# Router on the tokens between the two norms, first tile routed and half gathered before the second is made

## The chip, the cores and the metric

The kernel runs on one core of a Trainium2 chip. The metric is device microseconds of one execution, taken as the median of several runs. The core has a matrix engine (TensorE: PE for its matmuls, PEld for its weight loads), a vector engine (VectorE, DVE), a scalar engine (ScalarE, ACT), a general engine (GpSimd, POOL), a sync engine (SyncE, SP) that here issues nearly all transfers, and 16 DMA engines that carry them. Matmul results land in PSUM, which has 8 banks; everything else on the core lives in SBUF.

## The reference

Two layers over 256 tokens of width 1024. Each layer mixes tokens (attention of 8 heads beside a causal pooling mixer, one output projection), then runs a mixture of 16 experts:

```python
x = layer_norm_affine(DEEPNORM_ALPHA * x + g1 * y, ln1_g[l], ln1_b[l])      # "first norm"
h = layer_norm_plain(x) * (1 + sc2) + sh2                                   # "second norm"
...
scores = jax.nn.softmax((hf @ w_router).astype(jnp.float32), axis=-1)
sel = scores + router_bias
grp = sel.reshape(-1, N_EXPERT_GROUPS, EXPERTS_PER_GROUP)
best = jnp.argmax(lax.top_k(grp, TOP_K)[0].sum(-1), axis=-1)
...                                        # the two best experts of the best group, weights summing to 1
for e in range(N_EXPERTS):
    a = jax.nn.silu(hf @ w_gate[e]) * (hf @ w_up[e])
    y = y + gates[:, e:e + 1] * (a @ w_down[e])
```

`sh1, sc1, g1, sh2, sc2, g2` are the six parts of `silu(c) @ w_mod[l] + b_mod[l]`, called `mod` parts 0 to 5 below. A plain norm is (x - mean) / deviation per token, so the router's product with h is, per token, (x @ (sc * w) - mean * column sums of sc * w) / deviation + sh2 @ w, with sc = 1 + sc2.

## The kernel before

All weights are read once, 278.6 MB in pieces of 1 MB or less. `Stream` holds them in the order of use; `pump` issues the next piece on SP's queue whenever fewer than `limit` pieces are held, and `free` gives a piece back as soon as the matmul that uses it last is written down. The pieces live in a ring of 21 slots (`NS`) that also lends slots to scratch tiles: the rows `G`, `B` of the first norm, the normed tokens `xn2`, their transposes `xnT`. SP's queue works in order: an issue whose slot is still being read holds all that follow it.

Each engine works through its own list in the order in which the program was written (`manual_schedule`); engines wait for one another only for data and buffers. The tokens are two tiles `t` of 128. At the end of `mixer`:

- `out_mm(t)` is the output projection; the second tile's ends in two halves of 256 columns, and with its last columns the four `out` weight pieces are freed. `norms_of(t)` adds the residual, makes the first norm into `xt[:, t]` and the second into `xn2[t]`.
- `turn(t)` transposes `xn2[t]`, `logits(t)` multiplies by the router's weights, `exps(t)` sums the partial products and takes the exponentials.
- `xh`, `xl` are two parts of `xn2` whose sum is used in the gather, each for both tiles.
- `mod_mm(l, 5)` and `mod_mm(l + 1, 1)` (the latter in layer 0 only) multiply the condition by pieces of `w_mod`. They stand between `logits(0)` and `turn(1)`. `gate` (from `mod_fin(l, 5)`) runs `spread`: four matmuls and two ACT copies that lay the gate row over all partitions.

Then `router` runs `gate()`, makes the top-2 mask `M` of both tiles in one chain of small DVE operations, and places the tokens with three matmuls against a triangle (`posm`). `experts` makes one-hot tiles of 8 experts, gathers (`gather(0)`: 8 banks, four matmuls each, `xh` and `xl` of both tiles) and goes through eight pairs of experts: `gate_up`, `silu` (a tanh on ACT, two DVE products), `act_t`, `down`, `combine`. `warm(n)` is n matmuls of ones with no reader.

Layer 1 begins with `mod_mm(1, 0)`, whose weights come last in layer 0's stream; `mod_fin(1, 0)` then turns its result into columns, with a DVE sum that stands ahead of the DVE work on the second norm of the new layer (`ready`).

Of the kernel before, what the change touches and what calls it, by code (L numbers as in the profile page):

```python
# [8 lines left out]
F = mybir.dt.float32  # L9
BF = mybir.dt.bfloat16  # L10
# [6 lines left out]
D = 1024  # L17
# [56 lines left out]
def tile_trunk(ctx, tc, x, c, w_mod, b_mod, w_in, w_pool, pool_scale, w_out, ln1_g, ln1_b,  # L74
# [251 lines left out]

    def mod_fin(l, v):
        acc = macc.pop((l, v))
        part = s2()
        A.copy(part, acc)  # L330
        if v == 5:
            return lambda: spread(l, v, [(selm[:, n:n + 1], part) for n in range(2)])
        b = ps()
# [112 lines left out]
    def mixer(l, hT, xn, ready):  # L446
# [162 lines left out]

        py = [[], []]  # L610

        def out_mm(t):
            for n in range(2):
                last = t == 1 and n == 1
                for m in range(2 if last else 1):
                    c0, c1 = (256 * m, 256 * m + 256) if last else (0, 512)
                    py[t].append(ps())
                    for q in (2, 3, 0, 1):
                        w = st.get(("out", l, q))
                        for kk in range(2):  # L620
                            k = 2 * q + kk
                            T.matmul(py[t][-1][:, 0:c1 - c0], catT[:, k, t * 128:(t + 1) * 128],  # L622
                                     w[:, kk, n * 512 + c0:n * 512 + c1],
                                     start=(q == 2 and kk == 0), stop=(q == 1 and kk == 1))
                        if last and m:
                            st.free(("out", l, q))
# [6 lines left out]
        def norms_of(t):  # L633
            z = xn2[t]
            nb, wd = (4, 256) if t else (2, 512)
            bn = tiny.tile([128, nb, 6], F, name=f"bn{nb}")
            for j, (a, b) in enumerate(((0, 512), (512, 768), (768, D)) if t else ((0, 512), (512, D))):
                c0 = slice(a, b)
                V.tensor_mul(z[:, c0], py[t][j][:, 0:b - a], g1[:, c0])
                V.scalar_tensor_tensor(z[:, c0], xt[:, t, c0], ALPHA, z[:, c0], op0=OP.mult, op1=OP.add)  # L640
                for i in range(a // wd, b // wd):
                    V.bn_stats(bn[:, i, :], z[:, i * wd:(i + 1) * wd])
            affine(xt[:, t], z, z, G, B, stats_end(bn))

            mv, rs = stats(xt[:, t])
            V.tensor_scalar(z.rearrange("p (k q) -> p k q", k=8), xt[:, t].rearrange("p (q k) -> p k q", k=8),
                            mv[:, 0:1], rs, op0=OP.subtract, op1=OP.mult)

        def turn(t):
            for h in range(2):  # L650
                b = ps()
                for k in range(4):
                    T.transpose(b[:, k * 128:(k + 1) * 128], xn2[t][:, (4 * h + k) * 128:(4 * h + k + 1) * 128], ident)
                A.copy(xnT[:, 4 * h:4 * h + 4, t * 128:(t + 1) * 128], b.rearrange("p (k s) -> p k s", k=4))

        out_mm(0)
        norms_of(0)
        xh = big.tile([128, 2, D], FR, name="xn")

# [19 lines left out]
        A.copy(xh[:, 0], xn2[0])  # L679
# [3 lines left out]
        out_mm(1)  # L683

        bb = ps()
        for k in range(8):
            j = k % 4
            T.matmul(bb[32 * j:32 * j + 32, 0:1], wr[:, k, :], sh2[:, k:k + 1], start=(k < 4), stop=(k >= 4))
        rbias = const.tile([128, 1], F, name="rbias", bufs=1)
        A.copy(rbias, bb[:, 0:1])  # L690
        rpart = s2(S)

        def logits(t):
# [5 lines left out]
            A.activation(rpart[:, t * 128:(t + 1) * 128], bl[:, 0:128], AF.Identity, bias=rbias)  # L699

        xl = big.tile([128, 2, D], FR, name="hT")

        turn(0)
        logits(0)
        pl = ps()
        lg = [pl[:, t * 16:t * 16 + 16] for t in range(2)]
        ex = tiny.tile([128, 2, 16], F, name="r_ex", bufs=1)
        mx = tiny.tile([128, 2], F, name="r_mx", bufs=1)
        sm = tiny.tile([128, 2], F, name="r_sm", bufs=1)

        def exps(t):
            T.matmul(lg[t], rpart[:, t * 128:(t + 1) * 128], sel16[:, 0:NE], start=True, stop=True)
            V.tensor_reduce(mx[:, t:t + 1], lg[t], axis=AX.X, op=OP.max, negate=True)
            A.activation(ex[:, t], lg[t], AF.Exp, bias=mx[:, t:t + 1], accum_out=sm[:, t:t + 1])

        mod_mm(l, 5)
        gate = mod_fin(l, 5)
        if l + 1 < DEPTH:
            mod_mm(l + 1, 1)
        norms_of(1)  # L720
        exps(0)
        if l + 1 == DEPTH:
            warm(7)

        V.tensor_sub(xl[:, 0], xn2[0], xh[:, 0].bitcast(F))
        V.tensor_copy(xh[:, 1], xn2[1])
        V.tensor_sub(xl[:, 1], xn2[1], xh[:, 1].bitcast(F))
        turn(1)
        logits(1)
        exps(1)  # L730
        return xh, xl, (mx, ex, sm), gate
# [43 lines left out]
    def router(l, mes, gate):  # L775
        def tn(shape, name, dt=F):
            return tiny.tile([128] + shape, dt, name=name, bufs=1)

        mx, ex, sm = mes
        gate()  # L780
        warm(6)
# [431 lines left out]
```

## Time and profile before

| what | value |
|---|---|
| time, median of 3 runs | 725.13 us (724.12 to 725.71) |
| time of the profiled execution | 724.93 us |
| span of the profiled execution | 723.1 us |
| busy share PE / DVE / ACT / POOL | 94% / 45% / 17% / 7% |
| read from HBM | 278.59 MB, 387 GB/s over the span |
| output stage of the mixer to the first expert pair, layer 1 | 468.08 to 507.08 us |

The profiled execution's time is 1.8 us above its span and 0.2 us under the median. Layer 0 goes to about 366 us; the same stage of layer 0 lies 348.75 us before that of layer 1. A busy share is an average over stages with different limits, and a matmul's end is modelled, so a PE at 94% says little by itself.

### The profile page before, as it was taken

What the parts mean: (1) busy time and instruction counts of PE and PEld (TensorE: products, weight loads), DVE (VectorE), ACT (ScalarE), POOL (GpSimd) and SP (SyncE); (2) the same over time, 40 slices, a digit from 0 to 9 for tenths busy, and PEclk for the clock granted to TensorE, in tenths of its full rate; (3) what the DMA queues carried; (4) which work ended last, traced back from release to release, by engine and by line L of the source; (5) the groups of instructions that cost most, each with busy time, mean ns of one, the idle gap of its engine ahead of it and who ended that gap; (6) DMA issues with size and microseconds to landing.
All of it is one profiled execution on the core that took longest, in us unless ns stands there. A gap on an engine that the chain in (4) does not pass through costs nothing. (4 is left out here: it accounts for less than half of the span.)

```text
span 723.1 us, 8334 instructions
## 1 busy us (share of the span) xinstructions
PE 678.9 (94%) x3213; PEld 316.8 (44%) x3218; DVE 326.8 (45%) x582; ACT 124.8 (17%) x268; POOL 49.7 (7%) x76
## 2 busy tenths in 40 slices
PE   5999899999999999989979999998999999998994
PEld 2447555553333533423324575555333344342331
DVE  4008897662332532413153966666323243241305
ACT  1011432130110210121002035213210011012100
POOL 5001501100000000000010051010000000000002
PEclk9999999999999999999989999999999999999998
DMA  9999999999999999999999999767699999999992
GB/s 307 366 384 409 408 409 420 373 421 392 424 420 420 422 421 421 420 416 418 395 406 392 409 410 406 310 272 301 282 420 422 421 424 419 420 422 418 418 395 77
DMA packets 61729, 280.37 MB, mean 388 GB/s; under 512 B 5008, under 2 KB 14264, under 8 KB 38632
## 3 DMA queue, kind: packets, MB, share of 16 engines
q1 hardware_dynamic: 61040, 279.20, 96.1%
q8 instruction: 30, 0.49, 0.3%
q10 hardware_dynamic: 312, 0.32, 0.1%
q0 software_dynamic: 320, 0.14, 0.1%
q14 instruction: 27, 0.22, 0.1%
HBM read 278.59 MB, written 1.05 MB: 387 GB/s over the span
## 5 line engine op out<-in xcount | busy, mean ns | idle before, releaser
L918 PE MATMUL ps<-wr 128*64 128x512 f32 x1024 | 226.1, 596 | 0.0
L918 PEld LDWEIGHTS ps<-wr 128*64 128x64 f32 x1024 | 73.5, 138 | 147.2 <-issue 142.3
L960 PE MATMUL ps<-wr,s 128*64 128x512 f32 x512 | 113.8, 595 | 3.7 <-DVE s L945 2.9
L960 PEld LDWEIGHTS ps<-wr,s 128*64 128x64 f32 x512 | 35.5, 137 | 72.0 <-issue 63.8
L970 DVE SCALAR_TENSOR_TENSOR s<-ps,gc,gb 128x512 f32<-128x512 f32 x32 | 24.0, 748 | 84.0 <-PE ps L960 84.0
L455 PE MATMUL ps<-wr,hT 128*128 128x512 f32 x128 | 57.0, 597 | 0.4 <-ACT hT L429 0.2
L361 DVE SCALAR_TENSOR_TENSOR wr<-wr,condT 128x1024 f32<-128x1024 f32 x42 | 55.8, 1329 | 2.3 <-DMA wr<-in_w_mod_dram 0.9
L622 PE MATMUL ps<-wr,hT 128*128 128x512 f32 (+1 forms) x160 | 55.7, 507 | 0.1
L389 POOL TENSOR_TENSOR rs<-rs,mhalf 128x1 f32<-128x1 f32 x16 | 13.2, 823 | 554.1 <-DVE rs L388 554.1
L935 DVE TENSOR_TENSOR s<-s,ps 128x512 f32<-128x512 f32 x16 | 11.0, 687 | 86.5 <-PE ps L918 86.5
L973 ACT CAST wr<-s 128x512 fp32r<-128x512 f32 x30 | 18.5, 618 | 164.7 <-PE ps L918 107.7
L974 DVE TENSOR_TENSOR wr<-s,wr 128x512 fp32r<-128x512 f32 x30 | 20.8, 692 | 55.6 <-ACT wr L973 55.6
L622 PEld LDWEIGHTS ps<-wr,hT 128*128 128x128 f32 x160 | 30.2, 190 | 23.8 <-issue 21.5
L455 PEld LDWEIGHTS ps<-wr,hT 128*128 128x128 f32 x128 | 23.6, 190 | 28.9 <-issue 27.1
L984 PE MATMUL ps<-wr,sT 128*128 128x512 f32 x120 | 33.6, 413 | 0.0
L578 PE MATMUL ps<-wr,hT 128*128 128x512 f32 x64 | 28.3, 595 | 0.0
L504 PE MATMUL ps<-hT,wr 128*128 128x256 f32 x128 | 28.1, 380 | 0.0
L984 PEld LDWEIGHTS ps<-wr,sT 128*128 128x128 f32 x120 | 20.9, 189 | 16.3 <-issue 13.0
L933 DVE SCALAR_TENSOR_TENSOR s<-s,ps 128x512 f32<-128x512 f32 x16 | 11.0, 685 | 36.7 <-ACT s L932 36.7
L504 PEld LDWEIGHTS ps<-hT,wr 128*128 128x128 f32 x128 | 24.2, 190 | 4.5 <-issue 1.3
L876 PE MATMUL ps<-s,xn 128*128 128x512 f32 x64 | 25.4, 398 | 0.3 <-DVE s L854 0.3
L996 DVE TENSOR_TENSOR xt<-xt,ps 128x512 f32<-128x512 f32 x40 | 25.2, 683 | 0.5
(240 smaller groups left out, 611.5 us busy)
## 6 DMA issues: line engine op xcount, KB each, us to landing
wr<-in_w_gate_dram SPq DMA_DIRECT2D x64, 1024.0 KB, 19.3
wr<-in_w_up_dram SPq DMA_DIRECT2D x60, 1024.0 KB, 19.3
wr<-in_w_down_dram SPq DMA_DIRECT2D x56, 1024.0 KB, 19.5
wr<-in_w_mod_dram SPq DMA_DIRECT2D x48, 1024.0 KB, 15.1
wr<-in_w_in_dram SPq DMA_DIRECT2D x16, 1024.0 KB, 15.1
wr<-in_w_out_dram SPq DMA_DIRECT2D x8, 1024.0 KB, 18.7
wr<-in_w_down_dram SPq DMA_DIRECT2D x12, 512.0 KB, 11.1
wr<-in_w_up_dram SPq DMA_DIRECT2D x8, 512.0 KB, 17.4
```

What stands on the lines that cost most here:

```text
L361: V.scalar_tensor_tensor(acc, w[:, kk], condT[:, k, 0:1], acc, op0=OP.mult, op1=OP.add)
L455: T.matmul(pq[t][n], hT[:, k, t * 128:(t + 1) * 128], w[:, kk, n * 512:(n + 1) * 512], start=(k == 0), stop=(k == 7))
L504: T.matmul(pp[g // 2][:, (g % 2) * 256:(g % 2) * 256 + 256], w[:, kk, g * 128:(g + 1) * 128], hT[:, k, :], start=(k == 0 and g % 2 == 0), ...
L578: T.matmul(pv[t], hT[:, k, t * 128:(t + 1) * 128], w[:, kk, :], start=(k == 0), stop=(k == 7))
L622: T.matmul(py[t][-1][:, 0:c1 - c0], catT[:, k, t * 128:(t + 1) * 128], w[:, kk, n * 512 + c0:n * 512 + c1], start=(q == 2 and kk == 0), st ...
L876: T.matmul(b, xs[:, t, k * 128:(k + 1) * 128], SX[i][t], start=(n == 0), stop=(n == 3))
L918: T.matmul(bs[nm][64 * j:64 * j + 64, :], XE[i][k // 4][:, k % 4, c0:c0 + 64], st.get((nm, l, 2 * i + j, q))[:, k - k0, :], start=(k == 0) ...
L960: T.matmul(bo[n][64 * j:64 * j + 64, :], AT[i][:, k, 64 * j:64 * j + 64], st.get(("d", l, 2 * i + j, q))[:, k - k0, (n - n0) * 512:(n - n0 ...
L970: V.scalar_tensor_tensor(o, bo[n], GC[i], g2[:, c0], op0=OP.mult, op1=OP.mult)
L974: V.tensor_sub(ol[:, c0], o, oh[:, c0].bitcast(F))
L984: T.matmul(b, STt[i][:, t * 128:(t + 1) * 128], o[:, n * 512:(n + 1) * 512], start=(start and j == 0), stop=(stop and j == 1), skip_group_ ...
L996: V.tensor_add(b if i == NPAIR - 3 else xt[:, t, c0], xt[:, t, c0], b)
```

## The change

- `turn(t)` transposes `xt[:, t]` (between the norms) instead of `xn2[t]`. The logits are corrected afterwards by the token's mean and deviation: `bb` now has 32 small matmuls for two column sums, `crow` lays them over the partitions with two more, and `exps` has two more DVE operations.
- `out_mm(t, j)` does one part of the projection. After part 0 of the second tile come `turn(0)`, `logits(0)`, `exps(0)` and `route(0)` (the mask for one tile, 14 DVE operations); then part 1, `place(0)`, and part 2, which frees the `out` pieces.
- The first tile's share of the gather of the first four channel blocks (8 matmuls into four banks `gb0`) is done before `turn(1)`; `gather_first` does the remaining 24.
- `mod_mm(l + 1, 1)` and then `mod_mm(l, 5)` trade places; the latter stands behind `logits(1)`. `gate()` moves out of the router into the first expert pair, ahead of `silu(0)`. The two parts of the tokens (`X[t][:, 0]`, `X[t][:, 1]`) are made per tile.
- `warm` calls change: 7, 6 and 4 matmuls go, 8 (layer 1) and 2 come; the 8 at the start of layer 1 become 3.

```diff
+        PARTS = (((0, 512), (512, D)), ((0, 512), (512, 768), (768, D)))
...
+        X = [big.tile([128, 2, D], FR, name="xn"), None]
+        A.copy(X[0][:, 0], xn2[0])
+        V.tensor_sub(X[0][:, 1], xn2[0], X[0][:, 0].bitcast(F))
         mod_dve_fin(l, 3, acc[3])
         st.allow(NS - 3)
         sh2 = colt[l, 3]
-        out_mm(1)
...
+        out_mm(1, 0)
+        residual(1, 0)
...
         turn(0)
+        rsum = const.tile([128, 2], F, name="rbias", bufs=1)
+        bb = ps()
+        for i in range(2):
+            for k in range(8):
+                j = k % 4
+                T.matmul(bb[32 * j:32 * j + 32, i:i + 1], wr[:, k, :] if i else wrp[:, k, :],
+                         sh2[:, k:k + 1] if i else onesf, start=(k < 4), stop=(k >= 4))
...
         logits(0)
+        cb = ps()
+        for i in range(2):
+            T.matmul(cb[:, i * 16:i * 16 + 16], rsum[:, i:i + 1].to_broadcast([128, 128]), sel16[:, 0:NE],
+                     start=True, stop=True)
...
+        def exps(t, pl):
+            mv, rs = st2[t]
+            V.scalar_tensor_tensor(lgt[:, t], crow[:, 0], mv[:, 0:1], pl[:, 0:16], op0=OP.mult, op1=OP.add)
+            V.scalar_tensor_tensor(lgt[:, t], lgt[:, t], rs, crow[:, 1], op0=OP.mult, op1=OP.add)
+            V.tensor_reduce(mx[:, t:t + 1], lgt[:, t], axis=AX.X, op=OP.max, negate=True)
+            A.activation(ex[:, t], lgt[:, t], AF.Exp, bias=mx[:, t:t + 1], accum_out=sm[:, t:t + 1])
...
+        def place(t):
+            pb = ps()
+            if t:
+                T.matmul(pb[:, 0:16], ones, M[:, 0], start=True, stop=False)
+            T.matmul(pb[:, 0:16], tri, M[:, t], start=not t, stop=True)
+            V.scalar_tensor_tensor(posm[:, t], M[:, t], -OFF, pb[:, 0:16], op0=OP.mult, op1=OP.add)
+            return onehot_t(posm, 0, t)
+        exps(0, logit_mm(0))
+        route(0)
+        out_mm(1, 1)
+        residual(1, 1)
+        S0 = [place(0)]
+        out_mm(1, 2)
+        X[1] = big.tile([128, 2, D], FR, name="hT")
+        residual(1, 2)
+        first_norm(1)
+        gb0 = [ps() for _ in range(4)]
+        for k in range(4):
+            for i in range(2):
+                T.matmul(gb0[k], X[0][:, i, k * 128:(k + 1) * 128], S0[0], start=(i == 0), stop=False)
         if l + 1 < DEPTH:
             mod_mm(l + 1, 1)
+            part = mod_copy(l + 1, 1)
+        else:
+            warm(8)
         turn(1)
         logits(1)
+        pl = logit_mm(1)
+        st2[1] = mv, rs = stats(xt[:, 1])
+        exps(1, pl)
+        mod_mm(l, 5)
...
+        A.activation(o, i, AF.Identity, scale=rs, bias=nb)
+        A.copy(X[1][:, 0], xn2[1])
+        gate = mod_fin(l, 5)
+        route(1)
+        warm(2)
+        S0.append(place(1))
...
+        V.tensor_sub(X[1][:, 1], xn2[1], X[1][:, 0].bitcast(F))
...
+            bs = dict(enumerate(gb0))
+            for k in range(4):
+                part_mm(bs[k], 0, k, 1, 0, False, False)
...
                 most = nc.values_load(cnt[0:1, 16:17], min_val=0, max_val=S)
                 st.allow(NS - 2)
                 gated(0)
+                gate()
                 bs = scatter_t(0)
             silu(i)
...
                     mod_fin(l, 0)
-                    warm(8)
+                    warm(3)
```

## Rows read from the trace of the kernel before

**Rows 1.** The page, HBM traffic in 40 equal slices of the span

```profile
GB/s 307 366 384 409 408 409 420 373 421 392 424 420 420 422 421 421 420 416 418 395 406 392 409 410 406 310 272 301 282 420 422 421 424 419 420 422 418 418 395 77
```

**Rows 2.** Ten-microsecond windows: stretch, length, busy of five engines, PE clock, DMA share, GB/s

```profile
130.00:140.00 10.00, 9.63 (x100) 5.47 (x102) 6.95 (x14) 2.19 (x5) 1.56 (x2) 1.00 0.96 374
140.00:150.00 10.00, 8.57 (x66) 3.59 (x56) 7.40 (x20) 3.25 (x9) 0.50 (x1) 1.00 0.97 381
...
160.00:170.00 10.00, 10.00 (x48) 3.30 (x46) 3.38 (x12) 1.81 (x3) 0.00 (x0) 1.00 0.92 360
...
370.00:380.00 10.00, 7.51 (x34) 3.24 (x31) 4.06 (x12) 0.67 (x2) 1.53 (x2) 0.66 1.02 403
...
500.00:510.00 10.00, 10.00 (x46) 6.61 (x46) 4.63 (x12) 5.01 (x6) 0.00 (x0) 1.00 0.16 66
```

**Rows 3.** Waits of SP's queue in 110 to 136 us: total us, times, longest

```profile
SPq L56 <- PE ps L622: 11.7, 3, 10.7
```

**Rows 4.** Timeline of SP's queue, layers 0 and 1: start, us, issue

```profile
130.71 0.33 SPq L56 DMA_DIRECT2D wr<-in_w_up_dram  x1
...
510.76 0.33 SPq L56 DMA_DIRECT2D wr<-in_w_up_dram  x1
```

**Rows 5.** Timeline at the layer boundary, PE and DVE, with the idle time before

```profile
372.74 0.20 PEld L297 LDWEIGHTS ps<-wr,condT 128*32 128x32 f32 x8 [3.40 <-DMA wr<-in_w_mod_dram]
...
376.96 0.17 DVE L337 TENSOR_REDUCE col<-ps 128x8 f32<-128x16 f32 x1 [5.62 <-PE ps L335]
```

**Rows 6.** Timeline of layer 1, output projection to the first expert pair

```profile
468.08 13.94 PE L622 MATMUL ps<-wr,hT 128*128 128x512 f32 x48
...
481.95 0.31 PE L688 MATMUL ps<-col,wr__105 128*32 128x1 f32 x16
...
482.19 1.09 PE L653 MATMUL ps<-ident,wr 128*128 128x128 f32 x8
...
483.61 0.82 PE L697 MATMUL ps<-wr,wrp 128*32 128x128 f32 x16 [0.33 <-ACT wr L654]
...
485.52 1.29 DVE L399 SCALAR_TENSOR_TENSOR xt<-wr,rs 128x1024 f32<-128x1024 f32 x1 [0.44 <-POOL rs L389]
...
490.63 1.06 PE L653 MATMUL ps<-ident,wr 128*128 128x128 f32 x8 [0.92 <-DVE r_mx L713]
...
493.34 0.40 PE L712 MATMUL ps<-sel,s 128*128 128x16 f32 x2 [0.49 <-ACT s L699]
...
493.77 0.17 DVE L713 TENSOR_REDUCE r_mx<-ps 128x1 f32<-128x16 f32 x1 [0.21 <-PE ps L712]
...
494.38 0.17 DVE L782 RECIPROCAL r_sm<-r_sm 128x2 f32<-128x2 f32 x1 [0.43 <-ACT r_ex L714]
...
497.96 0.19 DVE L810 SCALAR_TENSOR_TENSOR r_M<-r_rk,r_fg 128x32 bf16<-128x32 f32 x1
...
498.71 1.29 DVE L854 TENSOR_TENSOR s<-slots,r_posm 128x512 fp32r<-128x512 f32 x2
...
499.51 0.19 PEld L876 LDWEIGHTS ps<-s,xn 128*128 128x128 f32 x1 [0.64 <-PE ps L283]
...
507.08 13.95 PE L918 MATMUL ps<-wr 128*64 128x512 f32 x64
```

**Rows 7.** Timeline of layer 1: the gate row, and silu's operations in the experts

```profile
493.59 2.18 PE L347 MATMUL ps<-s,selm 128*128 128x512 f32 x4
...
496.02 0.58 ACT L349 COPY gb<-ps 128x512 f32<-128x512 f32 x1 [0.49 <-PE ps L348]
...
521.11 0.69 DVE L935 TENSOR_TENSOR s<-s,ps 128x512 f32<-128x512 f32 x1 [5.49 <-PE ps L918]
...
537.54 0.60 ACT L932 ACTIVATE s<-ps 128x512 f32<-128x512 f32 x1 [0.78 <-PE ps L918]
```

**Rows 8.** Waits of PE's loads for transfers in 500 to 723 us: total, times, longest

```profile
PEld ps L918 <- DMA wr<-in_w_gate_dram: 1.1, 2, 0.8
...
PEld ps L960 <- DMA wr<-in_w_down_dram: 0.7, 3, 0.3
```

More of the change, by code (lines that the diff above doesn't have):

```diff
@@ L608, in mixer, with out_mm @@
         st.allow(NS - 6)
+        PARTS = (((0, 512), (512, D)), ((0, 512), (512, 768), (768, D)))
         py = [[], []]
[L612 to L626, printed above, removed]
+        def out_mm(t, j):
+            a, b = PARTS[t][j]
+            py[t].append(ps())
+            for q in (2, 3, 0, 1):
+                w = st.get(("out", l, q))
+                for kk in range(2):
+                    k = 2 * q + kk
+                    T.matmul(py[t][j][:, 0:b - a], catT[:, k, t * 128:(t + 1) * 128], w[:, kk, a:b],
+                             start=(q == 2 and kk == 0), stop=(q == 1 and kk == 1))
+                if t and b == D:
+                    st.free(("out", l, q))
         sc2, g1 = colt[l, 4], gb[l, 2]
@@ L682, in mixer @@
         sh2 = colt[l, 3]
-        out_mm(1)
[L685 to L690, printed above, removed]
+        out_mm(1, 0)
+        residual(1, 0)
         rpart = s2(S)
@@ L698, in logits @@
                          start=(k < 4), stop=(k >= 4))
-            A.activation(rpart[:, t * 128:(t + 1) * 128], bl[:, 0:128], AF.Identity, bias=rbias)
-        xl = big.tile([128, 2, D], FR, name="hT")
+            A.copy(rpart[:, t * 128:(t + 1) * 128], bl[:, 0:128])
         turn(0)
-        logits(0)
[L705 to L708, printed above, removed]
@@ L733, in rope, with onehot_t @@
+        return X, posm, S0, gb0, rest, gate
+    def onehot_t(posm, i, t):
+        e0 = 2 * i
+        Sx = s2p.tile([128, 8, 64], FR, name="s2")
+        V.tensor_tensor(Sx, slots[:, None, 0:64].to_broadcast([128, 8, 64]),
+                        posm[:, t, e0:e0 + 8, None].to_broadcast([128, 8, 64]), op=OP.is_equal)
+        return Sx.rearrange("p e s -> p (e s)")
     def rope(qk):
@@ L848, in onehot @@
         def onehot(i):
[L850 to L856 removed]
+            SX[i] = [onehot_t(posm, i, t) for t in range(2)]
         def gated(i):
@@ L1163, in ready @@
                 enter(l, t, hT, xn)
-        xh, xl, mes, gate = mixer(l, hT, xn, ready)
-        r = router(l, mes, gate)
-        ends, norm, norm_aside = experts(l, xh, xl, *r)
+        ends, norm, norm_aside = experts(l, *mixer(l, hT, xn, ready))
     rest = xt[:, 1, 512:D]
```

241 lines of the change are left out of this document (118 added, 123 removed).

## The prediction

> **What bounds the kernel now.** I read the page's traffic line first [rows 1]: in the expert stages the 16 DMA engines move 416 to 424 GB/s in nearly every slice, and the weights are 278.6 MB, so most of the run is as long as its transfers. Time is lost where traffic falls: at the ends, and in four slices of layer 1 (310, 272, 301, 282). The ten-microsecond windows show why the layers differ [rows 2]. In layer 1 the stretch just before the experts has 66 GB/s: the ring is full, the queue waits for a slot, and the first expert pair's matmuls set the next one free at 510.76 [rows 4]. Here compute sets the time. In layer 0 traffic hardly sags around the same stage: 374, 381 and 360 GB/s against 421 are losses of 1.1, 1.0 and 1.4 us. Layer 0 is bound by transfers, and the proof is where it ends: the last weights of its stream belong to the first product of layer 1, and PE's load waits 3.40 us for them while DVE waits 5.62 us for what PE makes of them [rows 5]. So three places count: what the change does to SP's queue in layer 0, to the chain before the experts in layer 1, and to PE in the experts of layer 1, where PE waits for transfers only 1.1 + 0.7 us in all [rows 8].
>
> **The second tile's projection comes later.** Before, PE does all of it in one run of 13.94 us and ends it at 482.0 [rows 6]. After, part 0 ends half-way, at 475.0, and then PE must do the transposes (1.09), twice the 0.31 of column products, the router's product (0.82), and three products like the L712 row (0.40 each): 3.7 us [rows 6]. Handing over to ACT and back (0.33, 0.49 in the same rows) I put at 0.6, so `logit_mm(0)` ends at 479.3. Part 1 takes a quarter of 13.94, 3.5, to 482.8. Meanwhile DVE works off two extra operations, the maximum with the exponential (493.77 to 494.38, 0.6) and 14 operations of routing. In the old chain 16 such operations take 494.38 to 498.15, 0.236 each; 14 are 3.3. From 479.3 that gives 0.5 + 0.6 + 3.3, the mask at 483.7. `place(0)` stands on PE ahead of part 2, so PE waits 0.9 us for it, and part 2 ends at 483.9 + 3.5 = 487.4: **5.4 us later** than before. Bounds: 4.3 without hand-over and wait, 6.2 if both are doubled in part.
>
> **Layer 0: SP's queue.** Part 2 frees the `out` slots. Before, the queue already waits for them, 10.7 us, the longest wait of that stretch [rows 3], until 130.71 [rows 4]; the first loss of 1.1 us is this. No other scratch tile is given back earlier by the change, so the issue moves to 136.1 and the DMA engines stand idle 5.4 us longer. They get back the later losses, 1.0 and 1.4, since a ring that is 5 us behind is no longer full there (the first slot from the experts comes at about 162, 510.76 less 348.75). Net +3.0 us. Bounds: 1.9 with the shortest shift, 5.4 if nothing is got back. The pieces of `mod_mm(l, 5)` are freed later too, but a piece of 1 MB takes 2.5 us at 421 GB/s, so the four `out` slots alone keep the engines busy for 10 us, and `mod_mm(1, 1)` frees four more within that time. At the layer boundary the weights arrive that much later, and PE and DVE wait already [rows 5], so the start of layer 1 moves by +3.0. PE itself comes there 3.9 us later (next parts); with 3.40 of wait and 3.0 of delay that stays hidden.
>
> **Layer 1: the chain to the experts.** From the end of the projection to the end of the first norm is 482.0 to 485.52 + 1.29 = 486.8 before [rows 6]; after, 487.4 + 4.8 = 492.2. The transposes can start there instead of waiting for the second norm (490.63): a delay of 1.6 where there was a gain of 3.8 to be had. From transposes to the maximum is 3.14, plus two operations 0.5: 495.8. Then 0.6 for the exponential, 3.3 for 14 operations: mask at 499.7. From the old mask (498.15) to the old gather's first load (499.51) is 1.36, so the gather starts at 501.1. It has 24 of 32 matmuls, three quarters of 499.51 to 507.08, 5.7: 506.8. The second one-hot of 0.65 (half of the L854 row) has gone ahead, and `mod_mm(l, 5)`, the second norm and the split of the tokens run beside the routing. **-0.3 us**. The later slots cost nothing in layer 1, where the queue stood still for most of the last 10 us before the experts (66 GB/s, [rows 2]). Bounds -1.5 and +0.6, with the shift above.
>
> **The first expert pair.** `gate()` had stood under the routing chain, which covered it; now nothing does. Its PE work starts when `gate_up(0)` ends, 507.08 + 13.95 = 521.0 in the old times [rows 6]. From its first matmul to the end of its second ACT copy is 493.59 to 496.60, 3.0 us [rows 7]. Written ahead of `silu(0)`, the copies hold the tanh on ACT; the tanh takes 0.60, the first product 0.69 like the second. The second product, at 521.11 before, starts at 521.0 + 3.0 + 0.6 + 0.7 = 525.3: +4.2 us for `act_t` and all that follows on PE. In layer 0 that is hidden at the boundary. In layer 1 PE can take it only from its waits for transfers, 1.8 us in all [rows 8], most of them late. So between +2.4 and +4.2; I take 2.6, near the lower end, as the waits lie behind the shift.
>
> In the Trainium skill, "TensorE: Matmul & The Clock Gate", section "Architectural detail: the array is 16× 32×32, not 1× 128×128", ACT's and DVE's queues are strictly first in, first out. By that rule the tanh cannot pass the two copies and the 4.2 stands; if it could pass, only PE's own 2.4 us of this part would be left, 1.8 of them covered, and the sum would be about 2 us lower. No row here shows ACT's order tested in that way.
>
> **Sum.** 3.0 - 0.3 + 2.6 = +5.3 us on 724.93, 730.2; the median lies 0.2 higher, so 730.4. The correction of the logits, the extra DVE split and the moved `mod_cols` are inside these chains or beside idle engines.
>
> **Rivals.** (1) *Faster: the first tile's detour costs the second tile nothing.* Place: PE between part 0 and part 2. Call its delay d. The terms are d - 2.4 at the boundary, d - 5.7 before the experts and 2.6 behind: 2d - 5.5. At d = 0 the first is held at -0.6 by PE's own arrival, and the time is 721.2. It decides from d = 2.0 down. Against it: PE's own work there adds up to 3.7 [rows 6]. Chance 0.12.
> (2) *Within 0.2%: both the queue's loss and the first pair's delay are hidden*, because slots come free elsewhere and layer 1's experts are after all bound by transfers. Then -0.3 is left, 724.8. Against it: [rows 3, 8]. Chance 0.12.
> (3) *Only one of them is hidden.* Without the queue's loss +2.3, 727.4; without the pair's delay +2.7, 727.8. For it: PE's waits are inferred from semaphores, and the waits of [rows 8] show that transfers and PE run close together in layer 1. Chance 0.14.
> (4) *The clock.* Between 370 and 380 the mean granted clock is 0.66 [rows 2]: about 6.8 us at 1.2 GHz, after PE had waited for the weights, and then it is at 2.4 GHz again. Five of the matmuls without a reader that follow go away, and PE idles there longer. If the low level lasts 4 us longer, the first products of layer 1 take twice their time: +2, 732.4. The first pair's new gap of 2 us may do the same. Chance 0.10.
> The Trainium skill, same page, section "What's actually happening", says that the throttled level is the default and that recent activity of PE releases it. The fall in rows 2 after a wait agrees; by that rule alone this rival would be the forecast, at 732.4.
>
> **Numbers.** The forecast has 0.52, the rivals 0.12, 0.12, 0.14 and 0.10. A difference under 0.2% (1.45 us) can't be told from none here. Faster 0.12, same 0.12, slower 0.76. For the range the lower end is 724.0, which leaves out rival 1 and a little of rival 2; the upper, 733.5, takes in d = 6.2 (+6.9) and the clock in part. The forecast's own range is 728 to 733.
>
> **What would show it.** Right: in layer 0 the window 130 to 140 falls under 250 GB/s and SP's longest wait there grows by some 5 us; the wait for `w_mod` at the boundary ends about 3 us later; in layer 1 the first `gate_up` starts 38.5 to 39 us after the projection; the first tanh starts after the copies of the gate row, and PE idles some 2 us before `act_t(0)`. Wrong: part 2 ends within 2 us of its old place; or PE in layer 1's experts shows as many waits for transfers as before; or the routing operations on half as wide tiles take much less than 0.236 each.

## The result, and the profile after

The changed kernel takes 733.92 us (median of 6 runs, 731.7 to 736.34) against 724.62 us for the kernel before (median of 6, 723.04 to 725.71): ratio 1.0132, 95% interval 1.0103 to 1.0162, or +9.6 us (the medians alone differ by 9.3). Forecast was +5.3, to 730.4; the measured time lies just above the range's upper end, 733.5. A second series gave 1.0133 (1.0109 to 1.0156). The profiled run took 733.28 us, with a span of 731.4 (before: 724.93 and 723.1).

HBM traffic of the changed kernel in 40 slices of the span, to be held against [rows 1]:

```profile
GB/s 306 365 385 409 409 408 419 246 419 420 419 420 420 419 420 418 419 414 417 397 407 391 409 409 417 332 120 412 363 368 420 419 419 419 420 419 416 416 351 58
```

The eighth slice has fallen from 373 to 246: a new hole, in layer 0. The ten-microsecond windows of the same kernel (columns as in [rows 2]):

```profile
120.00:130.00 10.00, 9.67 (x81) 5.77 (x80) 7.97 (x16) 2.79 (x7) 0.56 (x1) 1.00 0.93 382
130.00:140.00 10.00, 8.78 (x46) 6.77 (x49) 7.06 (x27) 0.40 (x2) 0.30 (x1) 1.00 0.38 138
140.00:150.00 10.00, 9.33 (x92) 3.49 (x85) 6.66 (x22) 4.85 (x8) 1.77 (x2) 1.00 1.01 424
160.00:170.00 10.00, 10.00 (x48) 3.29 (x46) 1.45 (x3) 0.00 (x0) 0.00 (x0) 1.00 1.01 419
370.00:380.00 10.00, 6.36 (x38) 1.27 (x38) 4.88 (x10) 0.59 (x1) 1.09 (x2) 0.83 1.02 408
530.00:540.00 10.00, 10.00 (x40) 3.22 (x42) 0.75 (x1) 0.35 (x1) 0.00 (x0) 0.83 0.82 322
```

The window 130 to 140 has 138 GB/s instead of 374: 6.7 us lost of ten. The window ahead of it has 382, where the kernel before had 421: 0.9 us. The two later losses of [rows 2] are gone (424 and 419 instead of 381 and 360). The clock at the boundary (370 to 380) is no lower than before, but in 530 to 540, in the first expert pair of layer 1, it now falls, and traffic with it. SP's wait in that stretch of layer 0, and the issue that ends it:

```profile
SPq L56 <- PE ps L626: 17.7, 4, 16.4
```

```profile
135.19 1.19 SPq L56 DMA_DIRECT2D wr<-in_w_up_dram  x2
```

Against [rows 3, 4]: 16.4 us instead of 10.7, to 135.19 instead of 130.71. The boundary, against [rows 5]:

```profile
376.81 0.20 PEld L297 LDWEIGHTS ps<-wr,condT 128*32 128x32 f32 x8 [2.40 <-DMA wr<-in_w_mod_dram]
...
380.51 0.17 DVE L343 TENSOR_REDUCE col<-ps 128x8 f32<-128x16 f32 x1 [5.32 <-PE ps L341]
```

The last weights come 4.07 us later, DVE's sum 3.55 later. Layer 1, PE, against [rows 6]:

```profile
471.56 7.03 PE L626 MATMUL ps<-wr,hT 128*128 128x512 f32 x16
...
481.41 3.70 PE L626 MATMUL ps<-wr,hT 128*128 128x256 f32 x16
...
486.33 0.17 PE L778 MATMUL ps<-r_M,tri 128*128 128x16 bf16 x1 [1.22 <-DVE r_M L770]
486.36 3.70 PE L626 MATMUL ps<-wr,hT 128*128 128x256 f32 x16
...
494.90 1.15 PE L659 MATMUL ps<-ident,xt 128*128 128x128 f32 x8 [1.24 <-DVE xt L405]
...
503.70 1.16 PE L915 MATMUL ps<-s,hT 128*128 128x512 f32 x4 [1.03 <-DVE s L842]
...
509.35 13.95 PE L983 MATMUL ps<-wr 128*64 128x512 f32 x64
```

From the projection's start to the first `gate_up` it is 37.8 us; before it was 39.0. PE then, and ACT beside it [rows 7], in the first pair:

```profile
523.24 1.12 PE L353 MATMUL ps<-s,selm 128*128 128x512 f32 x2
...
528.34 0.75 PE L1006 MATMUL ps<-ident,s 128*128 128x128 f32 x4 [2.25 <-DVE s L1000]
530.00 8.76 PE L1025 MATMUL ps<-wr,s 128*64 128x512 f32 x32 [0.91 <-DVE s L1010]
538.59 6.60 PE L983 MATMUL ps<-wr 128*64 128x512 f32 x30
```

```profile
524.61 0.59 ACT L355 COPY gb<-ps 128x512 f32<-128x512 f32 x1 [13.39 <-PE ps L354]
525.69 0.59 ACT L355 COPY gb<-ps 128x512 f32<-128x512 f32 x1 [0.49 <-PE ps L354]
526.17 0.60 ACT L997 ACTIVATE s<-ps 128x512 f32<-128x512 f32 x1
```

The tanh (L997) starts behind both copies of the gate row, PE idles 2.25 us before `act_t(0)`, and the first `down` takes 8.76 us where it took 7.09. The row of that `down` in the kernel before:

```profile
523.51 7.09 PE L960 MATMUL ps<-wr,s 128*64 128x512 f32 x32 [0.91 <-DVE s L945]
```

The waits of PE's loads for transfers in 500 to 733 us, against [rows 8], are 0.6 us instead of 1.8:

```profile
PEld ps L983 <- DMA wr<-in_w_gate_dram: 0.3, 1, 0.3
PEld ps L983 <- DMA wr<-in_w_down_dram: 0.3, 1, 0.3
```

**Four stretches.** PE's timeline cuts the run into four: from the products with v in layer 0 (L578 before, L584 after; the common start) to the second tile's projection in layer 1, from there to the first `gate_up`, from that to the second, and on to the end of the span. Before they are 389.0, 39.0, 23.35 and 192.7 us. All profiles of this study, as differences from these, with the measured ratio (up to the common start the runs differ by -0.3 to +2.7 us, 78.8 to 81.8, whichever the kernel):

```
kernel                         layer 0,   chain to   first   rest    ratio to before
                               boundary   experts    pair            (95%)
after                           +3.4       -1.2      +5.9    +0.1    1.0132 (1.0103-1.0162)
e13 after, once more            +5.2       -1.2      +5.9    +0.2    1.0133 (1.0109-1.0156)
e8  before, gate late           -0.4        0.0      +5.7    -0.4    1.0109 (1.0092-1.0126)
e2  gate behind silu            +4.4       +1.4      +1.2    -0.4    1.0088 (1.0069-1.0107)
e3  warm in the gap             +4.2       -1.2      +4.2    +5.7    1.0186 (1.0165-1.0208)
e1  gate early                  +3.7       +1.4       0.0    +0.8    1.0120 (1.0101-1.0140)
e7  early in layer 0 only       +3.9       -0.5       0.0    +1.2    1.0091 (1.0074-1.0108)
e6  early in layer 1 only       +1.6       -1.2      +5.2    +1.2    1.0143 (1.0121-1.0165)
e10 before, out held            +3.7        0.0       0.0    +0.1    1.0075 (1.0047-1.0104)
e9  before, slot taken          -1.6        0.0       0.0    +0.2    1.0012 (0.9992-1.0031)
e4  projection in one           +6.3       +3.9      +5.9    +0.1    1.0272 (1.0249-1.0294)
e5  logits alone                +2.9       +0.3       0.0    +3.2    1.0073 (1.0053-1.0094)
e11 logits, norm on DVE         +0.7       +0.7       0.0    +1.4    1.0062 (1.0039-1.0085)
e12 logits, split on POOL       +0.5       +0.8       0.0    +4.2    1.0099 (1.0071-1.0127)
e14 early reordered             +4.2       +3.3       0.0    +0.6    1.0135 (1.0110-1.0160)
e15 same, layer 1 only          +0.3       +2.7       0.0    +1.2    1.0109 (1.0080-1.0138)
e17 e14, ACT's order mended     +5.1       -2.7       0.0    +0.9    1.0042 (1.0026-1.0057)
e16 e15, ACT's order mended     +0.7       -2.7       0.0    +1.1    1.0017 (1.0001-1.0033)
```

The chain and the first pair repeat to 0.1 us where their code is the same, but for two: e2's chain and e6's pair, in which PE's clock fell at another place. The first stretch scatters by about 2 us. The last scatters by about 1, and is 3.2 to 5.7 us longer in e5, e12 and e3 (see the last section). The timed differences lie on average some 1.6 us above the sums of a row. On average 0.7 us of that is spent ahead of the common start; and the one profiled execution of the kernel before, 724.93 us, is slower than the medians of its own series, 723.06 to 724.62, by 0.3 to 1.9. Row by row the difference is between -1.2 and +3.6 us.

### The profile page after: what moved, and what is told of

It is laid out like the page before. It is cut to its first block, busy times and chain, and to the rows that moved or that the text cites. A ratio compares the mean times of both kernels' runs of the same rounds, so it can differ in the third digit from the quotient of the medians.

```text
span 731.4 us, 8420 instructions
## 1 busy us (share of the span) xinstructions
PE 678.7 (93%) x3238; PEld 316.5 (43%) x3238; DVE 329.0 (45%) x614; ACT 130.9 (18%) x276; POOL 49.8 (7%) x76
## 5 line engine op out<-in xcount | busy, mean ns | idle before, releaser
L1025 PE MATMUL ps<-wr,s 128*64 128x512 f32 x512 | 116.8, 609 | 4.0 <-DVE s L1010 2.9
L1025 PEld LDWEIGHTS ps<-wr,s 128*64 128x64 f32 x512 | 36.3, 140 | 74.6 <-issue 65.9
L1038 ACT CAST wr<-s 128x512 fp32r<-128x512 f32 x30 | 18.5, 618 | 166.8 <-PE ps L983 109.8
L584 PE MATMUL ps<-wr,hT 128*128 128x512 f32 x64 | 28.4, 597 | 0.0
L1013 ACT COPY s<-ps 128x512 f32<-128x512 f32 x12 | 7.0, 587 | 99.0 <-PE ps L1006 99.0
```

The source lines that it names most:

```text
L584: T.matmul(pv[t], hT[:, k, t * 128:(t + 1) * 128], w[:, kk, :], start=(k == 0), stop=(k == 7))
L1025: T.matmul(bo[n][64 * j:64 * j + 64, :], AT[i][:, k, 64 * j:64 * j + 64], st.get(("d", l, 2 * i + j, q))[:, k - k0, (n - n0) * 512:(n - n0 ...
L1038: A.copy(oh[:, c0], o)
```

## Experiments

### The gate row in the first pair: e8, e2, e3, e1

**e8**, the kernel before with this edit alone:

```diff
-        gate()
-        warm(6)
+        warm(16)
...
                 gated(0)
+                gate()
                 bs = scatter_t(0)
```

> The kernel before, with one edit of the change alone: gate() moved from the head of the routing into the first expert pair, ahead of silu(0); ten matmuls without a reader stand in its old place, so that PE stays as busy there. Theory: the first pair of layer 1 4.2 us longer, 1.7 more where the clock falls to 1.2 GHz behind the pause, at most 1.8 taken back from waits for transfers: +2.4 to +6 us, ratio 1.003 to 1.008. Rival (in layer 1's experts the transfers bound the time and hide it): 0.999 to 1.002.

Measured 1.0109, +7.9 us; in the profile the pair is 5.67 us longer and nothing else moves. PE of that run:

```profile
526.44 0.75 PE L940 MATMUL ps<-ident,s 128*128 128x128 f32 x4 [2.25 <-DVE s L934]
528.10 8.54 PE L959 MATMUL ps<-wr,s 128*64 128x512 f32 x32 [0.91 <-DVE s L944]
```

The same pause and the same slow `down` as in the changed kernel: this edit alone makes its third term; by the profile inside what was expected, by time 2 us above it. The rest of the run gets back 0.4 us, not 1.8 (more on that below).

**e2** keeps the call in the pair, but behind silu:

```diff
                 gated(0)
-                gate()
                 bs = scatter_t(0)
             silu(i)
             if i == 0:
+                gate()
                 scatter_e(0, bs)
```

> The changed kernel with gate() called in the first pair behind silu(0): the same work on PE and ACT at nearly the same place, but the tanh stands ahead of the two copies on ACT. Theory (the tanh held by the copies is the cost): PE makes the gate row while ACT and DVE make silu, act_t(0) comes some 3 us earlier, no pause: 728.5 to 730.5. Rival (it is PE's own 2.4 us of extra work, wherever it stands in the pair): 731.5 to 734.

Measured 1.0088, 729.86 us, inside what was expected; pair +1.2. ACT and PE:

```profile
520.60 0.60 ACT L997 ACTIVATE s<-ps 128x512 f32<-128x512 f32 x1 [5.29 <-PE ps L983]
529.10 0.59 ACT L355 COPY gb<-ps 128x512 f32<-128x512 f32 x1 [7.90 <-PE ps L959]
```

```profile
531.12 7.09 PE L1025 MATMUL ps<-wr,s 128*64 128x512 f32 x32 [0.52 <-DVE s L1010]
```

With the same operations, 4.6 of 5.9 us go. The order changed on ACT, and on PE too: the gate row's products now stand behind the four transposes of `scatter_t(0)`. But PE's own work is the same, so the cost was the tanh held by the copies, with the pause and the fall of the clock that came of it. (Its chain is 2.6 longer than the changed kernel's because PE's clock fell there: the products of `mod_mm(1, 5)` took 6.34 us instead of 3.64.)

**e3** leaves the hold and fills the pause:

```diff
                 gate()
                 bs = scatter_t(0)
+                warm(9)
```

> The changed kernel with nine matmuls without a reader (about 1.9 us) on PE behind scatter_t(0), in the pause that the copies make. Nothing else moves. Theory (the fall of the clock to 1.2 GHz behind the pause costs 1.7 us of the first down()): down() of the first pair 7.1 instead of 8.8 us, 731.5 to 732.8. Rival (the fall of the clock is the main cost of the first pair): 729 to 730.5. Rival (it costs nothing in the end): 733.5 to 734.5.

```profile
527.60 2.11 PE L283 MATMUL ps<-ones 128*128 128x512 bf16 x9
530.01 0.75 PE L1006 MATMUL ps<-ident,s 128*128 128x128 f32 x4 [0.31 <-DVE s L1000]
531.67 7.09 PE L1025 MATMUL ps<-wr,s 128*64 128x512 f32 x32 [0.91 <-DVE s L1010]
```

The pair is +4.2: `down` takes 7.09 again, so the fall of the clock is worth 1.7 and the hold 4.2. The time is nevertheless worse, 1.0186 (736.95 us, 731.5 to 732.8 expected), because of the last stretch (+5.7): PE's clock falls there (0.71 and 0.78 in 670 to 690), and PE stands 2.49 us for nothing that the profile shows. No expectation had that.

**e1** calls it in the mixer:

```diff
+        gate()
         route(1)
...
-                gate()
```

> The changed kernel with gate() called in the mixer just ahead of route(1), where the routing chain covers it, instead of in the first expert pair. Theory (the call in the first pair costs 4.2 us on PE, and the pause that it makes costs 1.7 us more by PE's clock): 733.9 - 5.9 = 728.0, at most 1.2 of it given back as waits for transfers, so 727.5 to 729.5; the first down() takes 7.1 us again. Rival (PE's waits for transfers in layer 1 hide the call, and the time lies in layer 0): 732.5 to 734.

Measured 1.0120, 731.87 us; 727.5 to 729.5 was expected. The pair is back to 23.35 exactly, but the chain is 2.6 longer: here the gate row's products wait for `mod_mm(l, 5)`, which the change had put last, and stand on PE ahead of `place(1)`. Of the 5.9 us that the pair gave, the chain took 2.6 and the last stretch 0.7, where PE now waits 0.89 us for weights. By its profile e1 is 2.3 us shorter than the changed kernel; the times do not show it clearly (1.0120 against 1.0132, with intervals that overlap).

### Layer 0 and the boundary: e7, e6, e10, e9

A flag chooses by layer between the early routing and the old order (projection in one run, both tiles routed together, `gate()` under the routing; the corrected logits in both):

```diff
+        SPLIT = l in (0,)        # e7; (1,) in e6; () in e5
```

> The other half: the first tile routed early in layer 0 only, layer 1 as in the run of the logits alone. Theory (the queue of layer 0): the boundary 3.5 to 5 us later than before, layer 1 to the experts 1 to 2.5 shorter, first pair as before: +1.5 to +4 us, ratio 1.002 to 1.0055. Rival (layer 0 is hidden, all of the loss sits in layer 1): 0.997 to 0.999.

> The changed kernel with layer 0 as in the run of the logits alone: the first tile is routed early in layer 1 only, and only there gate() stands in the first pair. Theory (the shift at the boundary comes from SP's queue in layer 0): the boundary as before, layer 1 to the experts 1.2 us shorter than before, first pair 4.2 us longer and 1.7 more where PE's clock falls: +3 to +5 us, ratio 1.004 to 1.007. Rival (the boundary is late for another reason, such as warm(3) or the moved columns of mod_mm(1, 1)): 1.009 to 1.013.

e7 measured 1.0091, e6 1.0143. Both fell by time. By stretches the split is clean: the boundary +3.9 with the early routing in layer 0 and +1.6 without, the pair +5.2 only in e6. The +1.6 stands beside a wait of SP's queue for the second tile's late split (`hT`), 8.1 us where the kernel before waits 2.8; e5 has it too. In e7 the chain is 0.5 shorter instead of 1 to 2.5, and the last stretch 1.2 longer, as long as its new wait for weights. By time both lie above what was expected, e6 by 5 us, of which its profile (729.7 us of span) shows 1.6 at the boundary and 1.2 in the rest; what the other runs of e6 lost can't be seen.

**e10** delays the last parts of the projection in the kernel before, by matmuls without a reader:

```diff
                 last = t == 1 and n == 1
+                if last and l == 0:
+                    warm(21)
```

> The kernel before, with 21 matmuls without a reader (4.5 us) ahead of the last two parts of the second tile's projection in layer 0 alone: the out slots, and all that stands behind on PE, come 4.5 us later; no routing is moved. Theory (the queue of layer 0 passes a later projection on to the boundary): the DMA engines stand idle 4.5 us longer near 130, of which later losses give back at most 2.4: boundary +2.1 to +4.5, ratio 1.003 to 1.0065. Rival (hidden by the ring): boundary within 0.5, ratio 1.000 to 1.001.

```profile
130.00:140.00 10.00, 10.00 (x65) 7.71 (x63) 2.00 (x6) 0.16 (x1) 0.00 (x0) 1.00 0.38 136
...
160.00:170.00 10.00, 10.00 (x47) 5.80 (x47) 5.67 (x14) 4.23 (x5) 0.00 (x0) 1.00 0.88 370
```

Measured 1.0075, the boundary +3.7, inside what was expected; the ratio lies above it by 0.001, less than its interval. A delay of 4.5 us alone makes the hole of the changed kernel in 130 to 140 (136 against 138 GB/s), and passes most of it on. The later losses stay here: 370 in 160 to 170 (360 in the kernel before, 419 in the changed one), and 391 in 170 to 180.

**e9** takes only the ring slot. In the changed kernel `turn(0)` stands ahead of the last use of the `out` weights, so `xnT` takes the slot of `acc[3]`, which before went to a piece of `w_up`:

```diff
-                        if last and m:
+                        if last and m and l:
                             st.free(("out", l, q))
...
         turn(0)
+        if l == 0:
+            for q in (2, 3, 0, 1):
+                st.free(("out", l, q))
```

> The kernel before, with one thing of the change alone: in layer 0 the scratch tile xnT takes the ring slot of acc[3], as it does in the changed kernel, because the out slots are given back behind turn(0) in the program's order (their last reader, and so their time, is the same). No instruction of PE, DVE or ACT moves. Theory (one piece of 1 MB stands 11 us later in SP's queue, so the DMA engines run dry 2.5 us earlier, and part of it is got back from the later losses of 1.0 and 1.4): boundary +0.1 to +2.5 us, ratio 1.000 to 1.0035. Rival (the slot costs nothing): boundary within 0.3.

```profile
130.00:140.00 10.00, 9.59 (x93) 5.97 (x95) 6.37 (x12) 1.60 (x4) 1.52 (x1) 1.00 0.73 286
...
160.00:170.00 10.00, 10.00 (x48) 3.37 (x49) 3.93 (x12) 2.84 (x4) 0.00 (x0) 1.00 1.02 413
```

Measured 1.0012 (0.9992 to 1.0031), no difference; the boundary is 1.6 us earlier in its profile, as neither theory had it, and within the scatter of that stretch. The hole is there (286 instead of 374 GB/s, 2.1 us, and 379 instead of 421 in the window ahead, 1.0), and the later losses of [rows 2] are gone (413 instead of 360): by itself the slot costs nothing that the time shows.

### The projection in one run: e4

```diff
-        out_mm(1, 0)
+        for j in range(3):
+            out_mm(1, j)
         residual(1, 0)
```

with the same order of the routing behind it.

> The changed kernel with the second tile's projection in one run, its three parts behind each other and ahead of the first tile's transposes, logits and routing; the out slots come free at their old time, and the scratch tile xnT takes one of them again. Theory (the later projection and the ring slot lost make the boundary 4 us later): the wait for w_mod at the boundary ends at 372 to 374, layer 1 from the projection to the experts is 0.5 to 2 us shorter, 727.5 to 730.5. Rival (the boundary is late because of PE's own work in layer 0): 732.5 to 734.

```profile
495.39 0.20 PE L779 MATMUL ps<-r_M,tri 128*128 128x16 bf16 x1 [4.48 <-DVE r_M L771]
497.53 3.59 PE L794 MATMUL ps<-s,xn 128*128 128x512 f32 x8 [1.95 <-DVE s L841]
```

Measured 1.0272, some 12 us above the expected range. The edit took the cover away, not the routing. PE now has nothing to do while DVE routes the first tile (4.48 + 1.95 us), the second tile's residual waits behind that on DVE, and in layer 0 `mod_mm(1, 1)` waits behind the early gather on PE, so that SP's hole only moves (51 GB/s in 140 to 150). It says nothing of what the detour costs where it stands; it shows that its place between the parts was the better of the two. PE's clock fell as well, in the first of the two waits.

### The corrected logits alone: e5, e11, e12

e5 is the flag above with no layer. e11 and e12 mend it:

```diff
+            o, i = in_rows(1)
+            V.tensor_scalar(o, i, mv[:, 0:1], rs, op0=OP.subtract, op1=OP.mult)
+            V.tensor_copy(X[1][:, 0], xn2[1])
+            V.tensor_sub(X[1][:, 1], xn2[1], X[1][:, 0].bitcast(F))   # e12: P.tensor_sub
             exps(1, pl)
```

In e12, in layer 1, `mod_mm(1, 5)` moves behind `logit_mm(1)` as well, and seven matmuls without a reader stand where it was.

> One part of the change alone: the router reads the tokens between the two norms and the logits are corrected, in both layers; but the second tile's projection stays in one run, both tiles are routed together behind it, nothing is gathered early, and gate() stays under the routing. Theory (what costs is the early routing of the first tile and the moved gate row, not the logits): no shift at the boundary; in layer 1 the transposes wait for the products of mod_mm(1, 5), at 20.7 us from the projection's start, instead of the second norm, at 22.5, and two operations of 0.25 come in: 1 to 2.5 us less than before, ratio to before 0.9965 to 0.9985. Rival (the correction, the extra split and the second norm on ACT cost as much as the wait for the norm): 1.000 to 1.004.

> The run of the logits alone once more, with the second norm of the second tile and its split on DVE ahead of exps(1), instead of on ACT and behind the one-hots. Theory (in that run the late split on DVE stood between the gather's evictions, 1.8 us, and gave the slot of xn2 back 5 to 8 us late to SP's queue): the gather 7.5 us again, SP's wait for the split gone, boundary -1 to +0.5, layer 1 to the experts 0.5 to 1.5 us shorter than before; ratio 0.9965 to 1.000. Rival (the corrected logits cost by themselves): 1.003 to 1.007.

> As the run before it, with two more edits: the low part of the split on POOL, and in layer 1 mod_mm(1, 5) behind the second tile's logits, so that its transposes start as the first norm ends. Theory: layer 1 to the experts 1.5 to 2.5 us shorter than before, the rest as before: ratio 0.9955 to 0.999. Rival (POOL's split comes late, or the gate row's products stand in the way of the mask): 0.999 to 1.004.

Measured 1.0073, 1.0062 and 1.0099; all three expectations fell. In e5 the late split holds a slot that SP waits for:

```profile
SPq L56 <- DVE hT L901: 9.6, 1, 9.6
```

In e11 that is gone and the boundary is within 0.7, but the chain is not shorter:

```profile
490.64 1.16 PE L659 MATMUL ps<-ident,xt 128*128 128x128 f32 x8
...
500.23 0.20 PE L825 MATMUL ps<-r_M,tri 128*128 128x16 bf16 x1 [2.75 <-DVE r_M L816]
```

The transposes start 20.25 us behind the projection's start (470.39) instead of 22.55, and PE then waits 2.75 us for the mask. The second norm, the copy and the split are still DVE's, and now stand ahead of the maximum. At the end of that wait PE's clock fell. In e12 the transposes start 18.8 us behind the projection's start, but the chain is 0.8 us longer than before. These two operations stand on the way to the maximum:

```profile
493.36 2.36 POOL L886 TENSOR_TENSOR hT<-wr,hT 128x1024 fp32r<-128x1024 f32 x1 [2.17 <-DVE r_lg L746]
493.36 2.38 DVE L747 SCALAR_TENSOR_TENSOR r_lg<-r_lg,rs,crow 128x16 f32<-128x16 f32 x1
```

DVE's operation on 16 elements starts with POOL's subtraction and ends with it: 2.38 us, where the same operation took 0.23 in e11. So the correction gave nothing in these runs: DVE had no room (e11), or stood 2.1 us longer on one operation beside POOL's (e12; why was not tried). The times say little of the chain, though: of the 6.4 us of e5's row 3.2 lie in the last stretch, and of e12's 5.5 us 4.2.

### The change in a better order: e13, e14, e15, e16, e17

e13 is the changed kernel again, as control. e14 keeps the early routing in both layers, e15 in layer 1 alone (layer 0 as in the kernel before). In both, the first tile's share of the gather moves as well, behind `logit_mm(1)`:

```diff
             exps(0, logit_mm(0))
             route(0)
-            out_mm(1, 1)
-            residual(1, 1)
-            S0 = [place(0)]
-            out_mm(1, 2)
+            for j in (1, 2):
+                out_mm(1, j)
+                residual(1, j)
...
             first_norm(1)
+            mod_mm(l, 5)
+            gate = mod_fin(l, 5)
+            S0 = [place(0)]
             turn(1)
             logits(1)
             pl = logit_mm(1)
...
+            gate()
             st2[1] = mv, rs = stats(xt[:, 1])
             exps(1, pl)
```

> The changed kernel itself, as the control of the two runs beside it on the same chip, and as a second profile. Theory (the three terms are of the program): layer 1's projection starts 3.5 to 5 us later than before, the experts start 37.8 us behind it, the second pair's products 29.2 us (27.6 if PE's clock stays) behind that: ratio 1.010 to 1.014. Rival (one of the terms was chance in one profile): one of the three stretches as in the kernel before, ratio under 1.009.

> The changed kernel with three moves, in both layers: PE goes on with part 2 of the projection at once instead of waiting for the first tile's mask (place(0) behind the first norm); the products of mod_mm(l, 5), and in layer 0 those of mod_mm(1, 1), directly behind part 2, where PE idles; gate() ahead of route(1). Theory: boundary 1.2 us earlier than in the changed kernel, +2.3 to +4 over before; layer 1 to the experts 36 to 37 us (before 39.0); pair 23.35 as before: ratio 1.000 to 1.002. Rival (the routing of the first tile costs elsewhere): 1.005 or more.

> The reordered early routing in layer 1 alone; layer 0 as in the kernel before, operation by operation. Theory (layer 0 is bound by SP's queue and can only lose by the change, layer 1 by the chain to the experts, which the change shortens once gate() and mod_mm(1, 5) are out of its way): boundary as before within 0.8, layer 1 to the experts 36 to 37 us against 39.0, pair 23.35: 2 to 3 us less than before, ratio 0.996 to 0.9975. Rival (what layer 1 gains there is lost behind it to transfers, since the ring has had less time to fill): 0.999 to 1.001.

e13 repeated all three terms (the boundary, +5.2, just above what was expected). e14 (1.0135) and e15 (1.0109) missed; ACT and PE of e15 show why:

```profile
500.26 0.59 ACT L355 COPY gb<-ps 128x512 f32<-128x512 f32 x1 [0.49 <-PE ps L354]
500.74 0.31 ACT L761 ACTIVATE r_ex<-r_lg,r_mx 128x16 f32<-128x16 f32 x1
```

```profile
504.36 0.17 PE L796 MATMUL ps<-r_M,tri 128*128 128x16 bf16 x1 [3.70 <-DVE r_M L788]
```

`gate()` had been written ahead of `exps(1)`, so its copies held the exponential on ACT, the same mistake as in the first pair. e16 and e17 move that line:

```diff
-            gate()
             st2[1] = mv, rs = stats(xt[:, 1])
...
             A.copy(X[1][:, 0], xn2[1])
+            gate()
             route(1)
```

> As the run with the early routing in layer 1 alone (e15), with one line moved: gate() behind ACT's second norm and copy of the second tile, instead of ahead of the maximum. Theory (in e15 the two copies of the gate row stood ahead of the exponential on ACT and held the routing of the second tile for 3.5 us, and PE's clock fell in the pause): layer 1 to the experts 36.3 to 37.5 us instead of 41.7, pair 23.35, the rest as in the kernel before: 1.5 to 3 us less than before, ratio 0.996 to 0.998, and 5 to 6 us less than e15. Rival (what layer 1 gains is lost behind it): 0.999 to 1.002.

> The same line moved in the run with the reordered early routing in both layers (e14). Theory: layer 1 as in e16, layer 0 still 3.4 to 5.2 us late at the boundary: +0.5 to +3 us, ratio 1.001 to 1.004. Rival (with the reordering layer 0 loses nothing): 0.996 to 0.999.

```profile
506.74 13.95 PE L1074 MATMUL ps<-wr 128*64 128x512 f32 x64
```

```profile
PEld ps L1074 <- DMA wr<-in_w_gate_dram: 2.9, 3, 2.1
PE ps L1074 <- DMA wr<-in_w_gate_dram: 1.3, 1, 1.3
PEld ps L1116 <- DMA wr<-in_w_down_dram: 0.5, 2, 0.3
```

e16: the chain is 36.3 us, as expected, 2.7 less than before, and the time is 1.0017 (1.0001 to 1.0033), the rival's. The rows above are its waits for transfers from 500 us on: its loads wait 3.4 us where they waited 1.8 [rows 8], and PE itself, which did not wait before, waits 1.3 us at one place, together with its load. Starting 2.7 us earlier, the experts of layer 1 meet a ring that is less full (argued, not tried); the rest is 1.1 longer and the boundary 0.7 later. By these columns 0.9 us of gain is left from the common start on, of which the time shows nothing. e17 is 1.8 us above e16 by time: what the early routing still costs in layer 0 (4.4 by the two profiles). No version here beats the kernel before.

## Why the prediction was wrong

The direction and the three places were right, and the sum was too small by about 4 us. The step that failed is **the first expert pair**, "between +2.4 and +4.2; I take 2.6, near the lower end": it measured 5.9, 5.9 and, alone, 5.7 (e8). It kept out of the sum what the pause costs by PE's clock (1.7 us), and it set waits for transfers off against the delay (1.6 of 4.2 us) that in the end gave nothing back.

**The second tile's projection.** Forecast 5.4 later. The rows give 486.36 + 3.70 - 471.56 = 18.5 us from start to end instead of 13.94, so 4.6. Between the end of part 0 (471.56 + 7.03) and part 1 (481.41) PE needed 2.8 us and not 3.7 + 0.6; its wait for the mask was 1.22 instead of 0.9. The forecast's lower bound of 4.3 leaves out the wait alone; without the hand-over too its own terms give 3.7.

**Layer 0.** Forecast +3.0, as 5.4 less 2.4 regained. Six profiles with this order gave 3.4 to 5.2, 4.1 in the mean. The later losses were regained (424 and 419 GB/s), but hardly for the reason given, that a late queue finds the ring less full: in e10, late by 4.5 us, they stay (370 and 391 GB/s), and 3.7 of the 4.5 come through. They go in e9 and in the changed kernel, where the ring slot is taken. "No other scratch tile is given back earlier by the change" overlooked the converse: a scratch tile is needed earlier, and `xnT` takes a slot that had carried 1 MB, 2.5 us of transfer. It shows ahead of the hole, in 120 to 130: 382 GB/s in the changed kernel and 379 in e9, against 421 before and 420 in e10. Against the kernel before, the windows of the changed kernel give 0.9 + 5.6 lost and 1.0 + 1.4 regained, +4.1. The slot is the missing term: 0.9 + 5.6 is 1.9 us more than the shift of 4.6. That the 2.4 came true was luck in part, as its reason did not hold alone. How the delay and the slot share the 4.1 is worked out from windows of one profile each, and the stretch scatters by 1.8 us with the same code.

**The chain.** Forecast -0.3, measured -1.2, inside its bounds. With the 4.6 of the projection in place of 5.4, the forecast's own terms (d - 5.7) give -1.1: this part was right.

**The first pair.** The 4.2 was right to 0.1 us (e3). Two things were not. The pause of 2.25 us on PE ended in 1.2 GHz, and `down` lost 1.7 us; that stood only in rival (4). And PE's waits for transfers gave nothing back on balance. The loads' waits fell from 1.8 to 0.6, and from the seventh pair's `down` to the end of the span it took 45.8 us instead of 47.2. But as much was lost just ahead of that, at the branch behind the seventh pair's gate products, so that the last stretch kept its 192.8 us. PE pauses at that branch in every profile. Here are the rows behind the pause, of the kernel before (its four products took 1.02), the changed kernel and e2:

```profile
666.30 7.09 PE L918 MATMUL ps<-wr 128*64 128x512 f32 x32
```

```profile
673.54 1.87 PE L414 MATMUL ps<-rowz,selz 128*128 128x512 bf16 x4 [2.25 <-PEq L1123]
675.34 7.77 PE L983 MATMUL ps<-wr 128*64 128x512 f32 x32
```

```profile
673.01 1.02 PE L414 MATMUL ps<-rowz,selz 128*128 128x512 bf16 x4 [2.25 <-PEq L1123]
673.97 7.94 PE L983 MATMUL ps<-wr 128*64 128x512 f32 x32
```

In the changed kernel the clock fell there, and the four products and the 32 behind them took 1.5 us longer. In e2 and e8 the clock stayed, and the 32 still took 7.94 and 8.04 us instead of 7.09, for a cause that no row shows. There the waits gave back 1.2 and 1.3 us behind the branch, of which 0.4 were left in the whole stretch.

In sum 4.1 - 1.2 + 5.9 + 0.1 = +8.9, against +9.6 measured.

**The rivals.** (1) fell: no d under 2. (2) and (3) fell: neither part was hidden. (4) was half right: the clock mattered, in the first pair and not at the boundary, where the 3 instead of 8 matmuls without a reader did no harm. The section of the Trainium skill that the prediction weighed ("TensorE: Matmul & The Clock Gate", "Architectural detail: the array is 16× 32×32, not 1× 128×128") calls ACT's queue strictly first in, first out. By that rule the 4.2 had to stand, and the runs agree: with only the order on ACT changed, the chain is 5.4 us shorter in e16 than in e15, and with the order on ACT and on PE changed, the pair is 4.6 shorter in e2 than in the changed kernel, what the clock lost in the pauses included.

## What to carry to other kernels

A moved operation takes its queue with it. Write beside each moved line what stands behind it on every engine that it uses: two copies of 0.59 us, ahead of a tanh or an exponential on ACT, cost 4.6 us (changed kernel against e2) and 5.4 (e15 against e16). Before shortening a chain, see what bounds the stage behind it: layer 0, where transfers set the time, only lost, and of a gain of 2.7 us in layer 1 1.1 came back as waits for weights and the time showed none. In a ring, needing a scratch tile earlier is a later transfer.

## What the runs showed that was not expected

PE's clock and its pauses decide by a few us, and not in the same way from one kernel to the next. The pause at the branch, 2.0 to 2.25 us in every profile, was followed by 1.2 GHz in some kernels and not in others, although their code there is the same. Up to there the last stretch is 134.8 to 135.0 us in every profile; from there to the next `down` it is 10.5 to 17.7, and behind that 45.8 to 48.4, longer where PE waits for weights. In five profiles PE stands still a second time, until 5 to 6 us behind the branch, for nothing that the profile shows: 1.6 us in e11, 1.67 in e6, 1.95 in e5, 2.49 in e3 and 3.75 in e12. That, with the clock, is the +5.7 of e3, whose code differs from the changed kernel's by nine matmuls in the first pair of each layer, and the +4.2 of e12. The cause stays open.

The timed runs of some kernels (e6, e15, e4, e8) lie 3 to 3.6 us above what their one profile shows beyond the kernel before. In e15, 2.7 us of that lie ahead of the common start; for the others it stays open.
